# Six taps of a depthwise convolution on ScalarE, summed by adding transfers, and the convolution norm's sums placed later

## The chip, the cores and the metric

The kernel runs on one core of a Trainium2 chip. The metric is the device time of one execution in microseconds (us). For the kernel before, three runs gave 868.67, 869.35 and 869.78 us; the median is 869.35. A further execution was recorded by the hardware profiler, and all profile lines come from it. The engines are called PE (TensorE; PEld is its weight load), DVE (VectorE), ACT (ScalarE), POOL (GpSimd) and SP (the queue that loads the weights).

## The reference

One decoder layer on 512 tokens of width 1024, in float32: a half-weighted SwiGLU feed-forward, a mixing part, and a second feed-forward. The mixing part projects the normalized input and splits it over three groups: sliding-window attention (8 heads of 64, window 128), a convolution group, and cross-attention into 256 memory tokens (4 heads). Their outputs are joined, multiplied by `w_out` and added to the input. The change is in the convolution group, which has 256 channels and 31 taps:

```python
def conformer_conv(u, w_dw, b_dw, g_ln, b_ln):
    a, gate = jnp.split(u, 2, axis=-1)
    h = a * jax.nn.sigmoid(gate)
    h = lax.conv_general_dilated(
        h, w_dw[:, None, :].astype(h.dtype), window_strides=(1,),
        padding=((CONV_WIDTH - 1, 0),), dimension_numbers=('NWC', 'WIO', 'NWC'),
        feature_group_count=CONV_CH) + b_dw
    return jax.nn.silu(layer_norm(h, g_ln, b_ln))
```

Per channel, the output at token t is the sum over the taps j of `w_dw[j]` times `h[t - 30 + j]`, plus a bias. The layer norm runs over the 256 channels.

## The kernel before

Activations are kept transposed: channels lie on the 128 partitions, the 512 tokens along the free axis. Each float32 matrix product is made of three matmuls on split operands (high x high, high x low, low x high). ACT writes the high part of each weight block and DVE the low part, from a buffer that SP's queue fills (the class `Weights`).

The mixing part is written out by hand. The string `ORDER` lists its steps; a loop calls them in that order. `pM0`, `pK`, `pS2` and so on project one tile of queries, keys or values; `sumX` and `facX` make the factors of the head norms; `scoresXj`, `softXj`, `weightsX`, `turnXj` and `valuesX` are one attention unit's parts; `outD_K` adds the products of output block D with the head pairs K. A list scheduler then orders the instructions on each engine, so steps that stand next to each other can interleave; each engine runs its own queue strictly in that order.

The convolution runs between these steps. The 256 channels are two halves (i = 0, 1) of 128 partitions. `glu(i, ...)` writes the gated input to `pad[:, i]`, with 30 zeros ahead of it (line 794 of the profile). `taps()` is a generator: its first call makes tap 0 of both halves (line 799), each later call one tap of both halves on DVE, `conv[:, i] = pad shifted by j * w + conv[:, i]` (line 805). The step `c` in `ORDER` calls it once by `pump(1)`. What is left is made at `ln_mean`, which calls `pump(TAPS)`.

The norm has four steps. `ln_mean` adds the two halves (line 1066), takes the mean over the channels by a matmul with a matrix of 1/256 (line 1068) and subtracts it (line 1070). `ln_square` squares on ACT (line 1076) and adds on DVE (line 1078). `ln_var` sums over the channels by matmuls of one column (line 1083), takes the reciprocal square root in small DVE operations and spreads it (line 1089). `ln_swish`, called after the third block of the next loop, transposes the spread factor (line 1037), multiplies (1095), applies the gain, the bias and the swish (1096) and splits the result (lines 972 and 973). `valuesS3`, the last step of `ORDER`, makes the last head pair's output (line 956).

A transfer that adds to its destination is there already in the feed-forward parts: four times in each, a product is scaled into a work tile on ACT and POOL's queue adds it to `x` (lines 504 and 505). Transfers of this kind are issued from POOL's queue; an engine that needs the sum waits for the landing. Softmax probabilities, turned by 90 degrees, lie in tiles from `pttile()`, a set of eight buffers of 128 x 512.

Of the kernel before, what the change touches and what calls it, by code (L numbers as in the profile page):

```python
# [34 lines left out]
AF = mybir.ActivationFunctionType  # L35
ALU = mybir.AluOpType
# [3 lines left out]
T = 512  # L40
# [6 lines left out]
TAPS = 31  # L47
# [4 lines left out]
C_BDW, C_GLN, C_BLN = 36, 38, 40  # L52
C_WDW = 42
# [9 lines left out]


ORDER = """
c c c c pM0 sumM0 pM1 sumM1 c c facM pK c scoresM00 scoresM01 c softM01 softM00 weightsM0 c sumK c pV scoresM11
scoresM10 turnM00 turnM01 softM10 c softM11 weightsM1 facK c valuesM0 normK turnV c ropeK c turnM10 turnM11
pS0 ropeS0 sumS0 pS1 sumS1 facA ropeS1 c valuesM1 pS2 scoresS01 scoresS00 softS00 softS01 c weightsS0 ropeS2 sumS2 c
pS3 scoresS10 softS10 scoresS11 out0_01 sumS3 out1_01 facB c turnS00 turnS01 softS11 scoresS20 c weightsS1 c c
valuesS0 turnS10 scoresS21 softS20 out1_2 ropeS3 softS21 c c turnS11 weightsS2 c valuesS1 scoresS30  # L70
turnS20 scoresS31 out0_2 softS31 turnS21 softS30 out2_0123 out1_3 weightsS3 c c out0_3 valuesS2 c c out3_0123 c
ln_mean ln_square turnS30 ln_var out4_0123 turnS31 out5_0123 valuesS3
""".split()
TILES = [s[1:] for s in ORDER if s[0] == "p"]

# [5 lines left out]
N_ACT = 20  # L81

SUM_BUFS = 3
MEM_F = 17
B_T3, B_Q1, B_Q2, B_T4, B_21, B_22, B_11 = range(7)


class Weights:
# [33 lines left out]
    def make_sums(self, i):  # L122
        nc = self.nc
        g, u = self.raw[i], self.raw[i + 1]
        s12 = self.extra.tile([P, 1024], F32, tag="sum", name=f"s12_{i}", bufs=SUM_BUFS)
        s43 = self.extra.tile([P, 1024], F32, tag="sum", name=f"s43_{i}", bufs=SUM_BUFS)
        l, r = slice(0, 512), slice(512, 1024)
# [56 lines left out]
    def next(self):  # L184
        i = self.at
        self.at += 1
        self.split_to(i + 1 + self.conv_ahead)
        return self.split.pop(i)
# [21 lines left out]
def layer(tc, ctx, a):  # L210
# [10 lines left out]
    def nm(s):  # L221
        uid[0] += 1
        return f"{s}_{uid[0]}"
# [172 lines left out]
    def ffn(pool, norm, first, gain, hooks, next_gain, last):  # L396
# [335 lines left out]
    hooks = {9 + i: [part] for i, part in enumerate(rotary())}  # L732
    hooks[MEM_F - 3] = [lambda: load(0), lambda: load(1)]
    hooks[MEM_F - 2] = [lambda: piece(0), lambda: piece(1), lambda: load(2), lambda: load(3)]
    hooks[MEM_F - 1] = [lambda: piece(2), lambda: piece(3)]
    hooks[MEM_F], hooks[MEM_F + 1] = [sums, p1], [p2]
    with tc.tile_pool(name="fast1", bufs=1) as pool:
        norm = ffn(pool, norm, STARTS, C_G1, hooks, C_GM, False)

    with tc.tile_pool(name="mix", bufs=1) as mix:  # L740
        norm = mixing(tc, nc, a, mix, W, norm, locals())
# [5 lines left out]
def mixing(tc, nc, a, mix, W, norm, e):  # L747
    PE, ACT, DVE, POOL = nc.tensor, nc.scalar, nc.vector, nc.gpsimd
    mm_bank, sc_bank, tp_bank, work, small = (e[n] for n in ("mm_bank", "sc_bank", "tp_bank", "work", "small"))
    par, ident, x, rb, rtok, rtok2 = (e[n] for n in ("par", "ident", "x", "rb", "rtok", "rtok2"))  # L750
# [8 lines left out]
    pad = mix.tile([P, 2, T + 32], F32, name="pad")  # L759
    conv = mix.tile([P, 2, T], F32, name="conv")  # L760
    kT = mix.tile([P, T], F32, name="kT")
# [16 lines left out]
    def pttile():  # L778
        return mix.tile([P, T], F32, tag="pt", name=nm("pt"), bufs=8)
# [8 lines left out]
    def glu(i, ps_a, ps_g):  # L788
# [4 lines left out]
        DVE.tensor_tensor(t2, ps_a, rb, op=ALU.mult)  # L793
        DVE.tensor_tensor(pad[:, i, 30 : 30 + T], t2, t, op=ALU.mult)

    def taps():
        w = lambda i, j: par[:, C_WDW + i * TAPS + j : C_WDW + i * TAPS + j + 1]
        for i in range(2):
            DVE.tensor_scalar(
                conv[:, i], pad[:, i, 0:T], w(i, 0), par[:, C_BDW + i : C_BDW + i + 1], op0=ALU.mult, op1=ALU.add  # L800
            )
        yield
        for j in range(1, TAPS):
            for i in range(2):
                DVE.scalar_tensor_tensor(conv[:, i], pad[:, i, j : j + T], w(i, j), conv[:, i], op0=ALU.mult, op1=ALU.add)
            yield

    tap = taps()

    def pump(n):  # L810
        for _ in range(n):
            next(tap, None)
# [29 lines left out]
    def rope(q):  # L842
        s = work()
        u = work()
        DVE.stream_shuffle(s, q, list(range(8, 16)) + list(range(0, 8)) + list(range(16, 32)))
        DVE.tensor_tensor(s, s, sinb, op=ALU.mult)
        DVE.tensor_tensor(u, q, cosb, op=ALU.mult)
        DVE.tensor_tensor(q, u, s, op=ALU.add)
# [156 lines left out]
    def sums(name, t, n):  # L1005

        if t == 0:
            v["st" + name] = small(8 * n)
        tile_name = name if name == "K" else GROUPS[name][t]
        head_sums(v["sq" + tile_name], v["st" + name][:, 8 * t : 8 * t + 8])  # L1010
# [49 lines left out]


    def ln_mean():
        pump(TAPS)
        both, avg = work(), work()[:, :P]
        POOL.memset(avg, 1.0 / 256.0)
        DVE.tensor_tensor(both, conv[:, 0], conv[:, 1], op=ALU.add)
        mean = tp_bank()
        PE.matmul(mean, avg, both, start=True, stop=True)
        for i in range(2):
            DVE.tensor_tensor(conv[:, i], conv[:, i], mean, op=ALU.subtract)  # L1070
# [20 lines left out]
    def ln_swish():  # L1091
# [7 lines left out]
    units = {"M0": 0, "M1": 1, "S0": 2, "S1": 3, "S2": 4, "S3": 5}  # L1099
    steps = {  # L1100
        "sumK": lambda: sums("K", 0, 1), "facK": key_factor, "normK": key_norm, "turnV": value_turn,
        "ropeK": lambda: rope(kT), "c": lambda: pump(1),
        "ln_mean": ln_mean, "ln_square": ln_square, "ln_var": ln_var,
    }
    for g, tiles in GROUPS.items():
# [127 lines left out]
```

## Time and profile before

| | |
|---|---|
| median of three runs | 869.35 us (868.67 to 869.78) |
| profiled execution, its time | 871.94 us |
| its span, first to last instruction | 870.1 us |
| mean granted PE clock | 0.998 |
| busy: PE, DVE, ACT, POOL | 862.3, 700.9, 446.3, 32.3 us |
| convolution taps on DVE (line 805) | 60 of 743 ns, from 390.0 to 491.8 us |
| the mixing part | about 376 to 545 us |

Times in the profile are counted from the first instruction of the span. In a timeline row stand the start, the time to the end of the last of the merged instructions, the engine, the line, the operation, what it writes and reads, the shape, and the count; in brackets, how long the engine idled before it and what ended that. Matmuls are pipelined: each is shown with its full time, so two that overlap both count, and a busy PE can still be waiting a little. In a group row the numbers behind the bar are the busy time in us and the mean of one in ns.

### The profile page before, as it was taken

How to read it: one execution, taken by the hardware profiler on the slowest of the kernel's cores; microseconds unless marked ns; L12 is line 12 of the kernel's file. 1: busy time of each engine (PE TensorE's matmuls, PEld its weight loads, DVE VectorE, ACT ScalarE, POOL GpSimd, SP SyncE). 2: the span in 40 equal slices, each digit the busy share in tenths (PEclk: the TensorE clock that was granted, in tenths of full speed). 3: DMA queues.
4: the chain of work that ended last, by engine and by line, in shares of the span. 5: the costliest groups of instructions: out<-in, count | busy, mean ns of one | idle time of the engine just before them, and what ended most of it. 6: DMA issues, size and time to landing. Idle time of an engine off the chain costs nothing.

```text
span 870.1 us, 14858 instructions
## 1 busy us (share of the span) xinstructions
PE 862.3 (99%) x5929; PEld 777.5 (89%) x5929; DVE 700.9 (81%) x1163; ACT 446.3 (51%) x739; POOL 32.3 (4%) x31
## 2 busy tenths in 40 slices
PE   9999999999999999999999999999999999999998
PEld 5889999999999998888777778889999999999998
DVE  7998878897888876769999876997987878787772
ACT  7455545454564444532949654454554444545540
POOL 0010000000120000300000021010000000000000
PEclk9999999999999999999999999999999999999999
DMA  7326334333334334222010412335334333324312
GB/s 272 121 83 166 94 96 133 98 99 120 121 122 145 107 108 131 73 96 61 13 49 13 134 56 91 98 90 161 100 111 121 98 113 90 115 96 117 103 49 98
DMA packets 34373, 90.60 MB, mean 104 GB/s; under 512 B 3200, under 2 KB 5760, under 8 KB 34304
## 3 DMA queue, kind: packets, MB, share of 16 engines
q1 hardware_dynamic: 32000, 85.99, 31.7%
q0 software_dynamic: 1152, 2.10, 1.5%
q10 hardware_dynamic: 1152, 1.57, 0.5%
q8 instruction: 46, 0.75, 0.3%
q14 instruction: 23, 0.19, 0.1%
HBM read 85.45 MB, written 2.10 MB: 101 GB/s over the span
## 4 chain that ended last, share of the span: by engine, by line
PE 95%; ACT 2%; DVE 1%; DMA 1%; issue 0%; SPq 0%; ACTq 0%
PE mm L350 15%; PE mm L349 15%; PE mm L351 15%; PE mm L446 11%; PE mm L448 11%; PE mm L447 11%; PE sc L446 2%; PE sc L448 2%; PE sc L447 2%; PE sc L349 1%; PE sc L350 1%; PE sc L351 1%; PE tp L956 1%; ACT p L907 1%; PE tp L942 1%; DMA x<-in_xT 1%
## 5 line engine op out<-in xcount | busy, mean ns | idle before, releaser
L446 PE MATMUL mm<-bh,whi 128*128 128x256 f32 x864 | 239.9, 278 | 0.0
L448 PE MATMUL mm<-bh,wlo 128*128 128x256 f32 x864 | 239.6, 277 | 0.0
L447 PE MATMUL mm<-bl,whi 128*128 128x256 f32 x864 | 239.6, 277 | 0.0
L169 ACT CAST whi<-wraw 128x1024 fp32r<-128x1024 f32 (+2 forms) x122 | 124.1, 1021 | 108.5 <-PE mm L350 48.8
L170 DVE TENSOR_TENSOR wlo<-wraw,whi 128x1024 fp32r<-128x1024 f32 (+2 forms) x122 | 145.2, 1192 | 35.3 <-ACT whi L169 34.9
L447 PEld LDWEIGHTS mm<-bl,whi 128*128 128x128 f32 x864 | 163.1, 189 | 0.7
L446 PEld LDWEIGHTS mm<-bh,whi 128*128 128x128 f32 x864 | 162.3, 188 | 0.7
L448 PEld LDWEIGHTS mm<-bh,wlo 128*128 128x128 f32 x864 | 162.2, 188 | 0.0
L351 PE MATMUL mm<-hh,wlo 128*128 128x256 f32 (+1 forms) x496 | 161.3, 326 | 0.0
L350 PE MATMUL mm<-hl,whi 128*128 128x256 f32 (+1 forms) x496 | 161.2, 326 | 0.0
L349 PE MATMUL mm<-hh,whi 128*128 128x256 f32 (+1 forms) x496 | 160.6, 326 | 0.0
L170 DVE TENSOR_TENSOR wlo<-s,whi 128x1024 fp32r<-128x1024 f32 x72 | 87.9, 1222 | 32.4 <-ACT whi L169 32.1
L351 PEld LDWEIGHTS mm<-hh,wlo 128*128 128x128 f32 x496 | 93.2, 188 | 9.2
L350 PEld LDWEIGHTS mm<-hl,whi 128*128 128x128 f32 x496 | 93.2, 188 | 8.0
L349 PEld LDWEIGHTS mm<-hh,whi 128*128 128x128 f32 x496 | 93.2, 188 | 7.9
L169 ACT CAST whi<-s 128x1024 fp32r<-128x1024 f32 x72 | 75.5, 1050 | 47.3 <-PE mm L447 43.5
L349 PE MATMUL mm<-xh,whi 128*128 128x512 f32 x192 | 76.2, 401 | 0.3 <-ACT whi L181 0.2
L350 PE MATMUL mm<-xl,whi 128*128 128x512 f32 x192 | 75.8, 395 | 0.5 <-DVE xl L361 0.5
L351 PE MATMUL mm<-xh,wlo 128*128 128x512 f32 x192 | 75.7, 394 | 0.0
L508 DVE SCALAR_TENSOR_TENSOR x<-mm,x 128x512 f32<-128x512 f32 x80 | 54.0, 683 | 4.0 <-PE mm L351 4.0
L169 ACT CAST vhi<-wraw 128x512 fp32r<-128x512 f32 x36 | 22.4, 622 | 59.6 <-PE sc L447 47.2
L467 ACT ACTIVATE t<-t 128x512 f32<-128x512 f32 x36 | 22.8, 633 | 56.3 <-DVE t L466 56.2
(243 smaller groups left out, 1378.8 us busy)
## 6 DMA issues: line engine op xcount, KB each, us to landing
wraw<-in_wgu SPq DMA_DIRECT2D x86, 512.0 KB, 3.5
wraw<-in_wd SPq DMA_DIRECT2D x44, 512.0 KB, 3.7
wraw<-in_win SPq DMA_DIRECT2D x12, 512.0 KB, 3.5
x<-t POOLq DMA_DIRECT2D x8, 256.0 KB, 6.2
out<-t SPq DMA_DIRECT2D x7, 256.0 KB, 2.0
x<-in_xT SPq DMA_DIRECT2D x3, 512.0 KB, 6.5
wraw<-in_wout_a SPq DMA_DIRECT2D x6, 256.0 KB, 2.7
wraw<-in_wgu SPq DMA_DIRECT2D x4, 256.0 KB, 4.9
```

The source lines that it names most:

```text
L169: nc.scalar.copy(hi[:, :cols], raw[:, :cols])
L170: nc.vector.tensor_tensor(lo[:, :cols], raw[:, :cols], hi[:, :cols].bitcast(F32), op=ALU.subtract)
L349: PE.matmul(ps[:, t], wh[:, w], hi(k)[:, t], start=one, stop=False, skip_group_check=cut > 1)
L350: PE.matmul(ps[:, t], wh[:, w], lo(k)[:, t], start=False, stop=False, skip_group_check=cut > 1)
L351: PE.matmul(ps[:, t], wl[:, w], hi(k)[:, t], start=False, stop=end, skip_group_check=cut > 1)
L446: PE.matmul(ps, wh[:, c], bh[k][:, block], start=one, stop=False, skip_group_check=not first)
L447: PE.matmul(ps, wh[:, c], bl[k][:, block], start=False, stop=False, skip_group_check=not first)
L448: PE.matmul(ps, wl[:, c], bh[k][:, block], start=False, stop=end, skip_group_check=not first)
L467: ACT.activation(g, g, AF.Silu)
L508: DVE.scalar_tensor_tensor(o, ps, 0.5, xd, op0=ALU.mult, op1=ALU.add)
L907: ACT.activation(self.p[n, h][:, c], src[h][:, i, c], AF.Exp, scale=self.fac[:, m : m + 1], bias=self.neg[:, m : m + 1], accum_out=self.de ...
L942: PE.transpose(ps[:, i * P : (i + 1) * P], self.p[n, h][:, c : c + P], ident)
```

## The change

Taps 0 to 5 of the second half go from DVE to ACT. Tap 0 with the bias is written to `conv[:, 1]`, tap 1 to a tile of the `pt` set; taps 2 to 5 are each written to a `pt` tile of their own and added by a transfer from POOL's queue, the even ones to `conv[:, 1]`, the odd ones to tap 1's tile. A fifth transfer adds that tile to `conv[:, 1]`. DVE's taps 6 to 30 of the second half then go on from `conv[:, 1]`. DVE's generator now yields single taps, first the whole first half and then the second; `c` takes two of them. A new step `a` makes one of ACT's taps; six `a` stand at the head of `ORDER`. At its end, `ln_square` stands behind `turnS30`, and `ln_var` behind `out5_0123`.

```diff
-c c c c pM0 sumM0 pM1 sumM1 c c facM pK c scoresM00 ...
+a a a c a c a a c c pM0 sumM0 pM1 sumM1 c c facM pK c scoresM00 ...
...
-ln_mean ln_square turnS30 ln_var out4_0123 turnS31 out5_0123 valuesS3
+ln_mean turnS30 ln_square out4_0123 turnS31 out5_0123 ln_var valuesS3
...
+N_ADDED = 6
...
     def taps():
-        w = lambda i, j: par[:, C_WDW + i * TAPS + j : C_WDW + i * TAPS + j + 1]
-        for i in range(2):
-            DVE.tensor_scalar(
-                conv[:, i], pad[:, i, 0:T], w(i, 0), par[:, C_BDW + i : C_BDW + i + 1], op0=ALU.mult, op1=ALU.add
-            )
-        yield
-        for j in range(1, TAPS):
-            for i in range(2):
-                DVE.scalar_tensor_tensor(conv[:, i], pad[:, i, j : j + T], w(i, j), conv[:, i], op0=ALU.mult, op1=ALU.add)
+
+        for i, j in [(0, j) for j in range(TAPS)] + [(1, j) for j in range(N_ADDED, TAPS)]:
+            w, src = tap_weight(i, j), pad[:, i, j : j + T]
+            if (i, j) == (0, 0):
+                DVE.tensor_scalar(conv[:, i], src, w, par[:, C_BDW : C_BDW + 1], op0=ALU.mult, op1=ALU.add)
+            else:
+                DVE.scalar_tensor_tensor(conv[:, i], src, w, conv[:, i], op0=ALU.mult, op1=ALU.add)
             yield

-    tap = taps()
+    def added_taps():
+
+        chains = [conv[:, 1], pttile()]
+        for j in range(N_ADDED):
+            w, src = tap_weight(1, j), pad[:, 1, j : j + T]
+            if j == 0:
+                ACT.activation(chains[0], src, AF.Identity, scale=w, bias=par[:, C_BDW + 1 : C_BDW + 2])
+            elif j == 1:
+                ACT.activation(chains[1], src, AF.Copy, scale=w)
+            else:
+                o = pttile()
+                ACT.activation(o, src, AF.Copy, scale=w)
+                POOL.dma_start(chains[j % 2], o, accum_op=ALU.add)
+            if j == N_ADDED - 1:
+                POOL.dma_start(chains[0], chains[1], accum_op=ALU.add)
+            yield
+
+    tap, added = taps(), added_taps()
...
-        pump(TAPS)
+        pump(2 * TAPS)
...
-        "c": lambda: pump(1),
+        "c": lambda: pump(2), "a": lambda: next(added, None),
```

POOL's queue, between the squares' sums ahead of the mixing part and the norm's matrix, has five new rows in the changed kernel (its lines lie up to 19 further down). What each waits for stands in brackets; `pt_4155` is tap 1's tile, DMASW is the landing of an earlier transfer of this queue:

```order
L822 DMA conv<-pt_4158 128x512 [waits Activation_49]
L822 DMA pt_4155<-pt_4163 128x512 [waits Activation_49]
L822 DMA conv<-pt_4168 128x512 [waits DMASW4_49,Activation_49]
L822 DMA pt_4155<-pt_4171 128x512 [waits DMASW5_49,Activation_49]
L824 DMA conv<-pt_4155 128x512 [waits DMASW7_49,DMASW6_49,DMASW0_49]
```

The third waits for the first, the fourth for the second, and the fifth for both of these.

DVE's queue at the factor of the memory queries (`facM`, the small operations on `qfac` and `s`), before:

```order
L334 TENSOR_SCALAR qfac_4250<-s_4198 128x16 [waits DVE_49]
L335 TENSOR_SCALAR s_4253<-s_4198 128x16
L805 SCALAR_TENSOR_TENSOR conv<-pad,par,conv 128x512
L337 TENSOR_TENSOR s_4254<-qfac_4250 128x16 [waits DVE_49]
L805 SCALAR_TENSOR_TENSOR conv<-pad,par,conv 128x512
L338 TENSOR_TENSOR s_4254<-s_4254,s_4253 128x16 [waits DVE_49]
```

And in the changed kernel:

```order
L335 TENSOR_SCALAR qfac_4266<-s_4214 128x16 [waits DVE_49]
L336 TENSOR_SCALAR s_4269<-s_4214 128x16
L807 SCALAR_TENSOR_TENSOR conv<-pad,par,conv 128x512 [waits DVE_49]
L338 TENSOR_TENSOR s_4270<-qfac_4266 128x16 [waits DVE_49]
L807 SCALAR_TENSOR_TENSOR conv<-pad,par,conv 128x512 [waits DMASW0_49]
L339 TENSOR_TENSOR s_4270<-s_4270,s_4269 128x16 [waits DVE_49]
```

The small operations keep their places. The tap between the first two products is now tap 6 of the second half, and it waits for the landing of the fifth adding transfer.

PE's queue at the end of `ORDER`, from the mean's matmul on. Before (`sc_5285` and `sc_5317` are the output blocks 4 and 5, the rows with `ident` are transposes):

```order
L1068 MATMUL tp_5234<-t_5230,t_5231 128x512
L942 MATMUL tp_5243<-ident,p_5130 128x128 x3
L942 MATMUL tp_5243<-ident,p_5104 128x128
L350 MATMUL mm_5211<-yl_3976,whi_5205 128x512
L351 MATMUL mm_5211<-yh_3968,wlo_5206 128x512
L349 MATMUL sc_5285<-yh_3968,whi_5279 128x512
L350 MATMUL sc_5285<-yl_3976,whi_5279 128x512
L942 MATMUL tp_5250<-ident,p_5104 128x128 x3
L351 MATMUL sc_5285<-yh_3968,wlo_5280 128x512
...
L1083 MATMUL tp_5256<-ones,t_5240 128x1 x4
```

And in the changed kernel, the rows ahead of the variance sums:

```order
L351 MATMUL mm_4856<-yl_3976,whi_5221 128x512
L961 MATMUL tp_5285<-ident,p_5149 128x128 x3
L961 MATMUL tp_5285<-ident,p_5123 128x128
L352 MATMUL mm_4856<-yh_3968,wlo_5222 128x512
L961 MATMUL tp_5292<-ident,p_5123 128x128 x3
L350 MATMUL mm_4875<-yh_3968,whi_5221 128x512
L351 MATMUL mm_4875<-yl_3976,whi_5221 128x512
L352 MATMUL mm_4875<-yh_3968,wlo_5222 128x512
L350 MATMUL mm_5164<-yh_3968,whi_5221 128x512
L351 MATMUL mm_5164<-yl_3976,whi_5221 128x512
L352 MATMUL mm_5164<-yh_3968,wlo_5222 128x512
L1102 MATMUL tp_5317<-ones,t_5263 128x1 x4
```

Before, 8 matmuls of 512 columns and 7 transposes stand between the mean's matmul and the variance sums; now 13 and 14. The mean's matmul now stands among the first products of output block 5, the variance sums behind the third of the next loop's blocks.

More of the change, by code (lines that the diff above doesn't have):

```diff
@@ L65 @@
 ORDER = """
-c c c c pM0 sumM0 pM1 sumM1 c c facM pK c scoresM00 scoresM01 c softM01 softM00 weightsM0 c sumK c pV scoresM11
+a a a c a c a a c c pM0 sumM0 pM1 sumM1 c c facM pK c scoresM00 scoresM01 c softM01 softM00 weightsM0 c sumK c pV scoresM11
 scoresM10 turnM00 turnM01 softM10 c softM11 weightsM1 facK c valuesM0 normK turnV c ropeK c turnM10 turnM11
@@ L794, in glu, with tap_weight @@
         DVE.tensor_tensor(pad[:, i, 30 : 30 + T], t2, t, op=ALU.mult)
+    def tap_weight(i, j):
+        return par[:, C_WDW + i * TAPS + j : C_WDW + i * TAPS + j + 1]
     def taps():
-        w = lambda i, j: par[:, C_WDW + i * TAPS + j : C_WDW + i * TAPS + j + 1]
-        for i in range(2):
-            DVE.tensor_scalar(
-                conv[:, i], pad[:, i, 0:T], w(i, 0), par[:, C_BDW + i : C_BDW + i + 1], op0=ALU.mult, op1=ALU.add
-            )
-        yield
-        for j in range(1, TAPS):
-            for i in range(2):
-                DVE.scalar_tensor_tensor(conv[:, i], pad[:, i, j : j + T], w(i, j), conv[:, i], op0=ALU.mult, op1=ALU.add)
-            yield
-    tap = taps()
+        for i, j in [(0, j) for j in range(TAPS)] + [(1, j) for j in range(N_ADDED, TAPS)]:
[4 more added lines that the diff above has]
+                DVE.scalar_tensor_tensor(conv[:, i], src, w, conv[:, i], op0=ALU.mult, op1=ALU.add)
+            yield
+    def added_taps():
[14 more added lines that the diff above has]
+    tap, added = taps(), added_taps()
     def pump(n):
@@ L1101, in mixing @@
         "sumK": lambda: sums("K", 0, 1), "facK": key_factor, "normK": key_norm, "turnV": value_turn,
-        "ropeK": lambda: rope(kT), "c": lambda: pump(1),
+        "ropeK": lambda: rope(kT), "c": lambda: pump(2), "a": lambda: next(added, None),
         "ln_mean": ln_mean, "ln_square": ln_square, "ln_var": ln_var,
```

## The prediction

> **What bounds the kernel now.** I read the page first, then TensorE's waits, then tables by stage (busy time of PE, PEld, DVE, ACT, POOL with counts, granted clock, share of the DMA engines, GB/s), and last the instructions around the places that the change touches.
>
> ```profile
> PE 862.3 (99%) x5929; PEld 777.5 (89%) x5929; DVE 700.9 (81%) x1163; ACT 446.3 (51%) x739; POOL 32.3 (4%) x31
> PE tp L1083 <- DVE t L1078: 1.4, 1, 1.4
> PE tp L956 <- ACT pt L945: 0.5, 2, 0.3
> 390.00:410.00 20.00, 20.00 (x107) 16.13 (x107) 18.82 (x37) 6.58 (x10) 0.00 (x0) 1.00 0.18 54
> 490.00:510.00 20.00, 18.06 (x101) 13.91 (x100) 12.40 (x28) 9.15 (x14) 0.00 (x0) 0.91 0.32 93
> ```
>
> TensorE sets the end: it is busy 99% of the span. A change on VectorE or ScalarE is therefore worth only what it takes from, or adds to, TensorE's waits. The longest of them in this part is the 1.4 us in which the convolution norm's variance sums (L1083) wait for VectorE's sum of squares (L1078). It lies in the only stage of the middle part with a granted clock under 1.0 (0.91 over 490 to 510 us). The instructions there, of TensorE and VectorE, and four stretches of 3.4 us:
>
> ```profile
> 482.99 1.75 PE L956 MATMUL tp<-pt,vtok 128*64 128x128 f32 x28
> 494.17 1.02 PE L1068 MATMUL tp<-t,t 128*128 128x512 f32 x2
> 495.92 1.27 DVE L1070 TENSOR_TENSOR conv<-conv,tp 128x512 f32<-128x512 f32 x2
> 498.49 0.69 DVE L1078 TENSOR_TENSOR t<-t,t 128x512 f32<-128x512 f32 x1 [1.30 <-ACT t L1076]
> 499.24 1.05 PE L1083 MATMUL tp<-ones,t 128*128 128x1 f32 x8 [1.41 <-DVE t L1078]
> 501.46 2.97 PE L956 MATMUL tp<-pt,vtok 128*64 128x128 f32 x28 [0.35 <-ACT pt L945]
> 495.00:498.40 3.40, 2.83 (x16) 2.00 (x14) 2.19 (x3) 2.06 (x4) 0.00 (x0) 1.00 0.92 264
> 498.40:501.80 3.40, 2.22 (x21) 1.98 (x23) 1.96 (x10) 1.03 (x3) 0.00 (x0) 1.00 0.26 104
> 501.80:505.20 3.40, 3.40 (x31) 3.04 (x27) 0.99 (x5) 0.71 (x2) 0.00 (x0) 0.50 0.02 5
> 505.20:508.60 3.40, 3.40 (x16) 2.51 (x15) 1.88 (x3) 2.79 (x3) 0.00 (x0) 1.00 0.00 0
> ```
>
> The reader is to see two losses. TensorE idles 1.41 us, then 0.35 us. Right behind a stretch with only 2.22 us of busy time out of 3.40 the clock is granted at 0.50 for 3.4 us, and the same 28 matmuls that took 1.75 us at 482.99 take 2.97. A half clock for 3.4 us costs 1.7 us of TensorE's time.
>
> **The change, part by part.** *The norm's sums are moved.* From the end of the mean's matmul (494.17 + 1.02 = 495.19) to L1083 at 499.24 the chain of two subtractions, two squares and a sum takes 4.05 us. In the new order 13 matmuls of 512 columns and 14 transposes stand between the two. The cadences come from these rows: one 512-column matmul starts 0.23 us after the other, and eight transposes take 0.87 us on the chain.
>
> ```profile
> 485.01 0.40 PE L349 MATMUL mm<-yh,whi 128*128 128x512 f32 x1
> 485.24 0.39 PE L350 MATMUL mm<-yl,whi 128*128 128x512 f32 x1
> 422.42 0.87 PE tp L942 x8
> ```
>
> 13 x 0.23 + 14 x 0.11 = 4.5 us, more than the 4.05: the wait of 1.4 us goes, and with it most of the 0.35 (I take 0.2). The next thing late is the last windowed head pair and the norm's own output: its values are followed at once by matmuls on their low part, which need a cast and a subtraction (some 0.5 us beyond the four matmuls ahead), and less work stands ahead of the norm's output than before. I give back 0.4 us. Idle time: -1.4 - 0.2 + 0.4 = -1.2. If the thin stretch is gone, the half clock is too: -1.7. Together **-2.9 us**.
>
> *Six taps leave VectorE.* They are six of these, spaced 0.66 us (five in 3.40):
>
> ```profile
> 398.53 3.40 DVE L805 SCALAR_TENSOR_TENSOR conv<-pad,par,conv 128x512 f32<-128x512 f32 x5
> 388.34 0.55 DVE L799 TENSOR_SCALAR conv<-pad,par 128x512 f32<-128x512 f32 x1
> 387.61 0.69 DVE L794 TENSOR_TENSOR pad<-t,t 128x512 f32<-128x512 f32 x1 [1.44 <-ACT t L791]
> ```
>
> That takes off 6 x 0.66 = 4.0 us of VectorE. Some of it comes back: the taps of one half now often follow one another, and a dependent instruction starts 0.04 us behind the end of the one before (387.61 + 0.69 = 388.30, then 388.34) where independent ones overlap by 0.08: 0.12 us more for each of some ten such places, 1.2 us. The rest, 2.8 us, pays for nothing by itself, since TensorE's waits hardly name VectorE; it is what lets the mean stand 14 matmuls earlier. If it were missing, the mean would be late instead.
>
> *Six ScalarE activations are added*, 0.71 us by the nearest row (0.82 for the one with a bias), spaced about 0.62 since ScalarE's activations overlap by 0.1. The second half of the padded input is written at 390.66 + 0.68 = 391.34, and ScalarE idles from there to 393.96:
>
> ```profile
> 390.66 0.68 DVE L794 TENSOR_TENSOR pad<-t,t 128x512 f32<-128x512 f32 x1
> 393.96 1.06 ACT L169 CAST whi<-wraw 128x1024 fp32r<-128x1024 f32 x1 [3.75 <-PE mm L350]
> 394.92 0.59 ACT L817 ACTIVATE t<-mm 128x512 f32<-128x512 f32 x1
> L360 ACT ACTIVATE xh<-x,par 128x512 fp32r<-128x512 f32 x8 | 5.7, 710 | 0.0
> L1096 ACT ACTIVATE conv<-conv,par 128x512 f32<-128x512 f32 x2 | 1.6, 816 | 0.2 <-DVE conv L1095 0.2
> ```
>
> All six end near 395.4. The square at 394.92 slips by 0.4 us, behind which VectorE already waited 1 us for TensorE's sums; I price it at 0. Without that idle stretch it would cost 3.8 us of ScalarE.
>
> *Five adding transfers of 256 KB, in two chains*, come onto POOL's queue; POOL runs nothing from 390 to 410 us. This is the term that decides. The last transfer adds one chain to the other, so three landings follow one another, and VectorE's tap 6 of the second half waits for the third. In VectorE's new order that tap stands between two small operations of a factor, where now a tap starts at 405.56:
>
> ```profile
> 405.47 0.16 DVE L337 TENSOR_TENSOR s<-qfac 128x16 f32<-128x16 f32 x1
> 405.56 0.74 DVE L805 SCALAR_TENSOR_TENSOR conv<-pad,par,conv 128x512 f32<-128x512 f32 x1
> 406.22 0.16 DVE L338 TENSOR_TENSOR s<-s,s 128x16 f32<-128x16 f32 x1
> 413.67 1.28 ACT L907 ACT_TABLE_LOAD   x1 [4.54 <-DVE neg L898]
> 408.04 1.03 PE L871 MATMUL mm<-mk,q 64*128 64x256 f32 x8
> 415.60 1.74 PE L871 MATMUL mm<-mk,q 64*128 64x256 f32 x8
> 418.67 1.13 PE L871 MATMUL sc<-mk,q 64*128 64x256 f32 x4
> ```
>
> Behind it on VectorE stand the factor, four maxima and the negated maxima (L898); for these ScalarE's softmax waits (4.54 us already), and for its exponentials TensorE's next scores: the eight matmuls at 415.60 take 1.74 us where eight at 408.04 take 1.03, so TensorE waits 0.7 us there already. No slack is left in that chain: each us that the transfer is late is a us of TensorE.
>
> The landing times come from the accumulating transfers of the feed-forward parts, the same size, kind and queue: all eight, then the first and the second of the group at 583 us alone.
>
> ```profile
> DMA to landing us min/median/max: 3.4/6.2/8.2
> DMA to landing us min/median/max: 3.4/3.4/3.4
> DMA to landing us min/median/max: 5.0/5.0/5.0
> 583.40 1.80 POOL L505 DMA_DIRECT2D x<-t  x2 [52.70 <-DVE bl L439]
> ```
>
> A transfer alone lands after 3.4 us, the second of a pair (issued 0.9 later) after 5.0, the third and fourth after up to 8.2, since four are queued there. Here two at most are in flight. The first addend is ready at 391.34 + 0.8 + 2 x 0.65 + 0.1 = 393.6; issues at 393.7 and 394.6; the second lands at 394.6 + 5.0 = 399.6; its successor meets one nearly finished transfer, so I take 3.7, nearer the lone row: 403.4; the last is alone: 403.5 + 3.5 = **407.0**, 1.4 us after 405.56. Bounds: 3.4 each gives 394.6 + 3 x 3.5 = 405.1, not late; 5.0 each gives 409.9, 4.3 late; the median 6.2 each gives 413.5, 7.9 late.
>
> *A second-order cost of that wait.* With 1.4 + 0.7 us, and the 0.6 us lost in the scores at 418.67 (four in 1.13 us, where eight took 1.03), the stretch around 416 would be about as thin as the one at 498.40 (1.76 us idle and small matmuls), behind which the clock was halved. I take +1.7; its bounds are 0 and 1.7.
>
> The Trainium skill ("TensorE: Matmul & The Clock Gate", Part 1) has the clock halved after a window of about 3.4 us in which the array idled. The row at 498.40 has 2.22 us of busy time in such a window and the next is still at 0.50, so here the page's rule is too mild; by the rule neither wait would halve the clock, and the new stall would come without its 1.7.
>
> Sum: -2.9 + 1.4 + 1.7 = **+0.2 us** on the profiled span of 870.1. That execution took 871.94, 2.6 above the median of the three runs shown (869.35); I carry the difference over unchanged: 869.5.
>
> **Rivals.** (1) *The transfers are in time.* For it: a lone transfer takes 3.4, and from 390 to 410 the DMA engines are a fifth busy. Against it: the pair's second took 5.0. Then nothing is paid: -2.9, 866.4. The Trainium skill ("DMA: Bandwidth & Descriptors", Anatomy of one DMA) fits such a transfer as about 2.0 us plus its bytes at 436 GB/s, an estimate of 2.6 us for 256 KB, by which the last would land near 402.7 and this rival would hold; none of the eight here landed under 3.4.
>
> (2) *The clock stays.* As the forecast, late by 1.4, but the stall falls across two of the clock's windows: -2.9 + 1.4 = -1.5, 867.9.
>
> (3) *The queue's latency decides: slower.* The second transfer of each pair waits for the first, as those at 583 us did, and all land after 5.0 or more. The tap is 4.3 us late, TensorE stops as long and loses a half clock: -2.9 + 4.3 + 1.7 = +3.1, 872.5; at the median, +6.7, 876.1. It decides from a lateness of about 3 us (landing behind 408.6). Against it: only two are in flight, and nothing else is on the queue.
>
> (4) *The norm's wait only moves.* If the transposes among the covering matmuls wait for their copies, or the mean itself is late since VectorE was, the 1.4 us and the half clock stay: without any lateness 0, with it up to +3.
>
> **How the numbers follow.** Forecast with its half clock 0.37; clock stays 0.12; in time 0.30; slow queue 0.16; norm unchanged 0.05. A measurement tells 0.2% (1.7 us) from no change: 867.6 to 871.1 is the same. Faster is rival 1 and some of rival 2 with a lateness under 1.2: 0.36. Slower is rival 3, half of rival 4 and the forecast's upper edge (late by over 3): 0.22. Same: 0.42. The range goes from rival 1 (866.4, less 0.2) to the slow queue with 5.0 each (872.5, plus 0.3), which leaves out the median-latency case and little else. The forecast's own range is 868 to 871.
>
> **What would show it.** Right: the wait of L1083 is under 0.3 us and the clock is 1.0 there; the fifth adding transfer lands about 1.4 us after VectorE is ready for tap 6, an idle time that names the adding transfer; TensorE's scores at some 417 wait about that much longer, with a granted clock of 0.5 behind them; the DMA view shows the new transfers at 3.4 to 5.0 us. Wrong: a landing before 405.6 (then rival 1), behind 408.6 (rival 3), full clock behind a stall of 1.4 us or more (rival 2), or an idle time of over 1 us that is still there ahead of the variance sums (rival 4).

## The result, and the profile after

The changed kernel takes 877.3 us (median of six runs, 875.33 to 881.49) where the kernel before, beside it, takes 868.1: ratio 1.0113, 95% interval 1.0087 to 1.0140. In a second comparison the ratio was 1.0082 (1.0058 to 1.0106). It is 7 to 9 us **slower**; the forecast was 869.5, with a range up to 872.8. The profiled execution took 879.11 us, with a span of 877.3.

The busy times on the page of the changed kernel moved by 5 us at most (PE +5.1 us, ACT +3.5, POOL +4.4, DVE -1.4), and do not say where the time went.

```profile
PE 867.4 (99%) x5929; PEld 781.0 (89%) x5929; DVE 699.5 (80%) x1157; ACT 449.8 (51%) x745; POOL 36.7 (4%) x36
```

TensorE's waits in the mixing part of the changed kernel say more (what waited and for what; total us, times, longest):

```profile
PE mm L890 <- ACT p L926: 3.1, 1, 3.1
PE mm L350 <- ACT yh L991: 1.6, 1, 1.6
PE tp L961 <- ACT p L948: 0.2, 1, 0.2
```

The 1.4 us ahead of the norm's variance sums is gone. In its place stand 3.1 us at the scores, for ScalarE's exponentials, and 1.6 us at the first matmuls that read the norm's output. By stage (busy time of PE, PEld, DVE, ACT, POOL with counts; granted clock, DMA share, GB/s), the changed kernel:

```profile
418.90:422.31 3.41, 1.44 (x6) 0.97 (x7) 3.41 (x10) 3.40 (x11) 0.00 (x0) 1.00 0.00 0
422.31:432.55 10.24, 10.24 (x27) 6.80 (x26) 7.38 (x21) 6.23 (x17) 0.00 (x0) 0.50 0.01 2
490.00:510.00 20.00, 20.00 (x139) 15.90 (x138) 16.91 (x39) 14.78 (x36) 0.00 (x0) 1.00 0.47 145
```

Behind a stretch in which TensorE was busy for 1.44 of 3.41 us, the clock is 0.50 for 10.24 us. In these TensorE is busy throughout at half the clock, so about half of them, 5.1 us, is lost. At the norm (490 to 510) the clock is 1.0 and nothing idles. TensorE's instructions that can be set against those of before:

```profile
416.31 0.40 PE L352 MATMUL mm<-xh,wlo 128*128 128x512 f32 x1
416.63 1.13 PE L890 MATMUL mm<-mk,q 64*128 64x256 f32 x4
420.87 1.13 PE L890 MATMUL mm<-mk,q 64*128 64x256 f32 x4 [3.11 <-ACT p L926]
424.12 2.07 PE L890 MATMUL sc<-mk,q 64*128 64x256 f32 x4
493.18 1.75 PE L975 MATMUL tp<-pt,vtok 128*64 128x128 f32 x28
517.71 1.19 PE L350 MATMUL mm<-yh,whi 128*128 128x512 f32 x4 [1.56 <-ACT yh L991]
```

Of the kernel before, one of these rows was shown, at 482.99; the two others:

```profile
415.27 0.40 PE L351 MATMUL mm<-xh,wlo 128*128 128x512 f32 x1
510.15 1.20 PE L349 MATMUL mm<-yh,whi 128*128 128x512 f32 x4 [0.34 <-ACT yh L972]
```

The last matmul of the value projection starts 1.04 us later than before (416.31 to 415.27). That comes from before the change: the matmuls of one column ahead of the mixing part, at 377.24 us, were at 376.10. The 28 value matmuls of the third pair are 10.19 late: the scores' stage cost **+9.15**. The first matmuls on the norm's output are 7.56 late: the norm's stage gained **2.63**. The eight scores at the stop take from 416.63 to 422.00 us, 5.37 us, where the eight at 415.60 took 1.74: 3.63 more. What is left of the 9.15, 5.5 us, comes behind them, nearly all of it the 5.1 us of the low clock; there, scores four at a time take 2.07 us where they took 1.13.

What TensorE waits for there is late because VectorE was. POOL's queue, VectorE and ScalarE in the changed kernel:

```profile
394.86 0.89 POOL L822 DMA_DIRECT2D conv<-pt  x1 [25.24 <-ACT pt L821]
395.48 1.17 POOL L822 DMA_DIRECT2D pt<-pt  x1
400.06 0.86 POOL L822 DMA_DIRECT2D conv<-pt  x1 [3.41 <-DMA conv<-pt]
402.19 0.86 POOL L822 DMA_DIRECT2D pt<-pt  x1 [1.26 <-DMA pt<-pt]
406.35 0.86 POOL L824 DMA_DIRECT2D conv<-pt  x1 [3.30 <-DMA pt<-pt]
409.67 0.75 DVE L807 SCALAR_TENSOR_TENSOR conv<-pad,par,conv 128x512 f32<-128x512 f32 x1 [2.95 <-DMA conv<-pt]
418.32 1.28 ACT L926 ACT_TABLE_LOAD   x1 [8.17 <-DVE neg L917]
```

VectorE waits 2.95 us for the fifth transfer. The softmax starts 4.65 us later than before (413.67 there), 3.6 beyond the offset of 1.04, which is what the scores lose at the stop.

### The profile page after: what moved, and what is told of

Same layout as the page of the kernel before. It is cut to its first block, busy times and chain, and to the rows that moved or that the text cites. A ratio compares the mean times of both kernels' runs of the same rounds, so it can differ in the third digit from the quotient of the medians.

```text
span 877.3 us, 14873 instructions
## 1 busy us (share of the span) xinstructions
PE 867.4 (99%) x5929; PEld 781.0 (89%) x5929; DVE 699.5 (80%) x1157; ACT 449.8 (51%) x745; POOL 36.7 (4%) x36
## 3 DMA queue, kind: packets, MB, share of 16 engines
q0 software_dynamic: 1872, 3.41, 2.4%
## 4 chain that ended last, share of the span: by engine, by line
PE 93%; DMA 2%; DVE 2%; ACT 2%; issue 1%; SPq 0%; POOL 0%; POOLq 0%; ACTq 0%
PE mm L350 15%; PE mm L351 15%; PE mm L352 15%; PE mm L449 11%; PE mm L447 11%; PE mm L448 11%; PE sc L449 2%; PE sc L447 2%; PE sc L448 2%; PE sc L350 1%; PE tp L961 1%; PE sc L351 1%; PE sc L352 1%; DMA pt<-pt 1%; PE sc L890 1%; DMA x<-in_xT 1%
```

## The experiments

Two executions of one and the same kernel differ in the first feed-forward part: the last value-projection matmul of the changed kernel started at 416.31 in one trace and at 411.32 in another. So besides the ratio, each table row below has the time from that matmul to the end of the span, in one profiled execution, against the 454.8 us of before (870.1 - 415.27).

| kernel | ratio to before (95%) | from the scores to the end |
|---|---|---|
| changed, second comparison | 1.0082 (1.0058 to 1.0106) | +7.5 |
| norm's order alone | 1.0024 (1.0008 to 1.0039) | +2.1 |
| taps alone | 1.0051 (1.0037 to 1.0065) | +5.7 |
| no joining transfer | 1.0048 (1.0030 to 1.0065) | +6.6 |
| extra matmuls in the stop | 1.0040 (1.0026 to 1.0055) | +3.3 |
| own buffer, old norm order | 0.9986 (0.9969 to 1.0003) | -3.6 |
| own buffer, new norm order | 0.9987 (0.9972 to 1.0003) | -3.6 |
| one chain, new norm order | 0.9981 (0.9966 to 0.9995) | -2.6 |
| four taps, old norm order | 1.0036 (1.0017 to 1.0056) | +5.1 |
| one chain, old norm order | **0.9952 (0.9934 to 0.9970)** | -4.3 |

**Theory** after the first traces: the wait for the last landing, and the low clock behind it, are the loss; the norm's part is a gain. **Rivals**: the added work on ScalarE and the DMA engines is the loss; or the moved sums are.

### The norm's order alone

```diff
 # the kernel before
-ln_mean ln_square turnS30 ln_var out4_0123 turnS31 out5_0123 valuesS3
+ln_mean turnS30 ln_square out4_0123 turnS31 out5_0123 ln_var valuesS3
```

> The kernel before with the new order of the norm's steps alone: all taps stay on VectorE, no adding transfer. Theory (the move of the sums is a gain of its own, the added taps are the loss): the 1.4 us wait of the variance sums and the half clock behind it go, 2.9 us less, ratio 0.9967; granted clock 1.0 between 490 and 510 us. Rival (the move needs the lighter VectorE, or the wait only moves): within 1 us of before, ratio 0.999 to 1.001, with an idle time of over 1 us still ahead of the variance sums or a stretch at 0.5 behind them.

Measured: 1.0024, **slower by 2.1 us**. TensorE's three longest waits in the mixing part of this kernel:

```profile
PE mm L349 <- ACT yh L972: 2.7, 1, 2.7
PE tp L1037 <- DVE t L1089: 1.1, 1, 1.1
PE tp L1083 <- ACT pt L945: 0.6, 1, 0.6
```

The wait for the square is gone, and the later variance makes its factor (L1089) late by 1.1 and the norm's output (L972) by 2.7 us. The half clock moved too (by stage, the same kernel):

```profile
508.77:512.18 3.41, 3.41 (x10) 2.65 (x9) 1.74 (x4) 0.73 (x1) 0.00 (x0) 0.50 0.09 23
```

So the theory's gain does not come from the order. The rival of the prediction, that the wait only moves, holds for this part by itself.

### The taps alone

```diff
 # the changed kernel
-ln_mean turnS30 ln_square out4_0123 turnS31 out5_0123 ln_var valuesS3
+ln_mean ln_square turnS30 ln_var out4_0123 turnS31 out5_0123 valuesS3
```

> The changed kernel with the norm's steps back in their old order: the six taps by ScalarE and adding transfers stay. Theory (late chain and clock are the loss): the 3.1 us stop of TensorE ahead of its scores and the half clock behind it stay; the 2.6 us that the norm's move gained are lost: 9.2 + 2.6, about 12 us slower than before, ratio 1.0135. Rival (the move of the sums costs, the taps are harmless): not slower than before, ratio under 1.002. Rival (ScalarE's and the DMA engines' added work spread over the whole stage is the loss): about as slow, but with no wait of TensorE over 2 us at the scores.

Measured: 1.0051, 4.4 us slower, and not the 12 expected. TensorE in this kernel:

```profile
415.44 2.07 PE L890 MATMUL mm<-mk,q 64*128 64x256 f32 x4 [3.02 <-ACT p L926]
489.20 1.75 PE L975 MATMUL tp<-pt,vtok 128*64 128x128 f32 x28
496.94 1.02 PE L1087 MATMUL tp<-t,t 128*128 128x512 f32 x2
502.15 1.05 PE L1102 MATMUL tp<-ones,t 128*128 128x1 f32 x8
512.02 1.08 PE L350 MATMUL mm<-yh,whi 128*128 128x512 f32 x4
```

The stop at the scores is the same, 3.02 us. But in the norm's stage TensorE no longer waits at all: from the 28 value matmuls to the first on the norm's output it gains 6.21 - 1.87 = **4.3 us** on the kernel before, where the changed kernel gained 2.6. The chain from mean to variance is as long as ever (497.96 to 502.15, 4.19 us, where it was 4.05); what changed is that the mean's matmul stands earlier, 7.74 us behind the row of the value matmuls (496.94 - 489.20) where it was 11.18 (494.17 - 482.99), since VectorE has six taps less to do ahead of it (it is 11.19 with the new order alone and 7.75 in the changed kernel, so the taps do it, not the order); more of the output matmuls are left to fill the chain. The order alone (+2.1) and the taps alone (+4.4) add up to 6.5, about the 7.1 of the second comparison.

### Without the joining transfer

```diff
 # the changed kernel
+    late = rb
...
-        chains = [conv[:, 1], pttile()]
+        chains = [conv[:, 1], late]
...
-            if j == N_ADDED - 1:
-                POOL.dma_start(chains[0], chains[1], accum_op=ALU.add)
...
 def ln_mean():
+    DVE.tensor_tensor(conv[:, 1], conv[:, 1], late, op=ALU.add)
```

(`rb` is the spread factor of the norm ahead of the mixing part, not needed any more here.)

> The changed kernel without the fifth adding transfer (the one that joins the two chains): the second chain is added by one VectorE sum ahead of the mean. All six activations and four of five transfers stay. Theory (only the wait for the last landing costs, and the half clock that it brings): VectorE's first tap of the second half now needs only the first chain, whose second landing came some 2 us before VectorE was ready; the stop of TensorE shrinks to the 0.7 us of before, no half clock there, and the gain at the norm is left: 2 to 3 us less than before, ratio 0.9965 to 0.998, some 11 us less than the changed kernel. Rival (the added ScalarE work and the transfers cost by themselves): still over 5 us slower than before. A first chain that lands late by its own would show as an idle time of VectorE that names it.

Measured: 1.0048, 4.2 us slower than before and some 3 us better than the changed kernel, not 11. By itself that is nearer the rival. The trace shows why it does not decide: VectorE and TensorE in this kernel (here the scores are L889):

```profile
399.35 1.42 DVE L808 SCALAR_TENSOR_TENSOR conv<-pad,par,conv 128x512 f32<-128x512 f32 x2 [2.33 <-DMA conv<-pt]
415.39 1.98 PE L889 MATMUL mm<-mk,q 64*128 64x256 f32 x4 [2.17 <-ACT p L925]
```

The landing comes earlier, but so does the tap that waits: the scheduler reckons with the landing and now puts it as the 11th of VectorE's taps instead of the 15th. VectorE idles 2.33 us instead of 2.95, TensorE 2.17 instead of 3.11, and 13.65 us at 0.50 follow. Four of its seven runs had a mean clock of 1.0 and still took 869.2 to 873.4 us, so the low clock is not its whole loss. What counts is then the landing *against the place of the tap that waits*, which the kernels below test.

### Extra matmuls in the stop

```diff
 # the changed kernel, in scores()
+N_BUSY = 14
...
-            for i in range(2):
+            busy = not self.win and self.t == 1 and j == 1
+            if busy:
+                junk = tp_bank()
+            for i, h in [(i, h) for h in range(2) for i in range(2)] if busy else [(i, h) for i in range(2) for h in range(2)]:
                 n = 2 * j + i
                 c = self.cols(n)
-                for h in range(2):
+                if busy and (i, h) == (0, 1):
+                    for _ in range(N_BUSY):
+                        PE.matmul(junk, xhk(0)[:, :P], xhk(0), start=True, stop=True)
...
```

The edit also puts these scores in order of the head, so that the four of the first head stand ahead of the extra matmuls.

> The changed kernel with 14 extra matmuls of 512 columns (3.2 us, their result is not used) on TensorE in the middle of the scores that wait, so that the wait of 3.1 us is as long as before but TensorE is not idle in it. The landing is as late as in the changed kernel. Theory (two losses: a wait of 3.1 us, and a half clock of three windows, 5.1 us, that TensorE's idleness brings): the extra matmuls cost nothing, the half clock goes or shrinks to one window: 3.4 to 6.8 us less than the changed kernel, ratio to before 1.0035 to 1.0075. Rival (the low clock has another cause, or the slow scores are slow because ScalarE is late): no gain, ratio 1.0105 or more, with stretches at 0.5 still between 415 and 435 us.

Measured: 1.0040, 3.6 us less than the changed kernel, with 3.47 us of work added. TensorE, and then the stages, of this kernel:

```profile
418.31 3.47 PE L893 MATMUL tp<-xh 128*128 128x512 f32 x14
421.71 1.13 PE L897 MATMUL mm<-mk,q 64*128 64x256 f32 x4
423.62 0.70 PE L897 MATMUL sc<-mk,q 64*128 64x256 f32 x2 [0.78 <-ACT p L933]
```

```profile
418.90:425.74 6.84, 5.66 (x25) 3.68 (x23) 6.84 (x20) 6.83 (x19) 0.00 (x0) 1.00 0.00 0
425.74:432.57 6.83, 6.01 (x24) 5.24 (x23) 6.83 (x17) 4.77 (x12) 0.00 (x0) 0.50 0.01 2
```

The stop is filled, the low clock comes 3.4 us later and lasts two windows of 3.41 us, not three or four. All runs bear this out: five of these six have a mean clock of 0.996, which is two windows, where eleven of the changed kernel's twelve have 0.992 or 0.994. Waiting and low clock are two losses, and the second follows from the stop. It is not gone, since the smaller waits behind (0.78, 0.40, 0.82 us) remain.

### The landing taken out of the queue, with both orders of the norm

```diff
 # the changed kernel; once with the norm's old order, once with the new
+    late = rb
...
+            elif (i, j) == (1, N_ADDED):
+                DVE.tensor_scalar(late, src, w, None, op0=ALU.mult)
             else:
-                DVE.scalar_tensor_tensor(conv[:, i], src, w, conv[:, i], op0=ALU.mult, op1=ALU.add)
+                acc = late if i else conv[:, 0]
+                DVE.scalar_tensor_tensor(acc, src, w, acc, op0=ALU.mult, op1=ALU.add)
...
 def ln_mean():
+    DVE.tensor_tensor(conv[:, 1], conv[:, 1], late, op=ALU.add)
```

> The changed kernel with the norm's steps in their old order, and with VectorE's taps of the second half in a buffer of their own; the chain of ScalarE's taps is added to them by one VectorE sum ahead of the mean. All six activations and all five transfers stay, but no tap waits for a landing. Theory (the wait for the last landing and the half clock behind it are the loss, the lighter VectorE is a gain at the norm, the new order costs 2 us): no stop at the scores over the 0.7 us of before, no idle time at the norm; the 4.4 us gained there in the kernel with the taps alone, less up to 0.7 for the extra sum: 3.5 to 4.5 us faster than before, ratio 0.995 to 0.996. Rival (the added work on ScalarE and on the DMA engines is the loss): 3 to 5 us slower than before, as with the taps alone.

> The same buffer of its own for VectorE's taps of the second half, with the norm's new order. Theory: as the kernel with the old order, but 1.6 to 2 us slower, since the norm's output is late for the last matmuls (an idle time of 1 to 2 us that names the split of the norm's output): 1.5 to 2.9 us faster than before, ratio 0.9965 to 0.998. Rival (the new order is a gain as predicted, 1.2 us of idle time): faster than the kernel with the old order.

Measured: 865.87 and 866.61 us where before has 868.68; ratios 0.9986 and 0.9987, just short of certain. All six activations and all five transfers are still there, and nothing is lost by them: the rival of the added work falls. TensorE at the scores (here L894), with the old norm order:

```profile
414.48 1.13 PE L894 MATMUL mm<-mk,q 64*128 64x256 f32 x4 [0.65 <-ACT p L930]
```

The stop is 0.65 us, and this execution had no low clock. It is on the edge: of the twelve runs of the kernel with the old order, eight granted a mean clock of 1.0 and took 865.0 to 866.1 us; four granted 0.992 to 0.994 and took 869.0 to 871.2. A mean of 0.994 is three windows at half speed, as in the trace of the changed kernel. Between the two norm orders nothing is to be told here; the scheduler placed other work differently as well, and both have a last wait of 0.2 us. The expected 1.6 to 2 us did not show, and the 3.5 to 4.5 us of gain expected with the old order shows on the trace (-3.6) and not in the ratio, which includes the runs with a low clock.

### One chain instead of two

```diff
 # the changed kernel
-                POOL.dma_start(chains[j % 2], o, accum_op=ALU.add)
+                POOL.dma_start(chains[0], o, accum_op=ALU.add)
```

> The changed kernel with all four adding transfers into the first chain, so that five landings follow one another instead of three: at 3.4 us and 0.45 to the next issue each, the last lands near 414 us instead of 409.6, and VectorE's tap, one operation later in its order, waits about 7 us instead of 2.95. Theory (each us of lateness is a us of TensorE): the stop at the scores grows from 3.1 to about 7 us, the stretch at 0.5 behind it stays 10 to 14 us: 4 us slower than the changed kernel, ratio to before 1.012 to 1.016. Rival (lateness does not set the end, the added work does): as slow as the changed kernel within 1 us.

Measured: 0.9981, **faster**, where 4 us more were expected. The landings came even later than reckoned; POOL's first and last issue and VectorE in this kernel:

```profile
390.92 0.89 POOL L822 DMA_DIRECT2D conv<-pt  x1 [25.26 <-ACT pt L821]
409.13 0.86 POOL L824 DMA_DIRECT2D conv<-pt  x1 [3.22 <-DMA conv<-pt]
410.81 0.23 DVE L917 TENSOR_TENSOR neg<-s,qnfac 128x4 f32<-128x4 f32 x2
412.45 1.41 DVE L807 SCALAR_TENSOR_TENSOR conv<-pad,par,conv 128x512 f32<-128x512 f32 x2 [0.66 <-DMA conv<-pt]
```

From first to last issue it is 18.2 us, where the changed kernel took 11.5 (394.86 to 406.35): 6.7 us more, where 4.4 were reckoned. But the scheduler, seeing the long chain, put the tap that waits *behind* the maxima and the negated maxima (L917). The expectation had assumed a place one operation later; the tap went six taps later. A landing 7 us later, counted from the first issue, costs nothing: TensorE's scores, 2.02 us for eight, no longer wait for it. That is the clearest answer to the prediction's "each us that the transfer is late is a us of TensorE". What TensorE still waits for in the mixing part is the norm's output, 1.3 us.

### Four taps

```diff
 # the changed kernel, with the norm's old order
-N_ADDED = 6
+N_ADDED = 4
```

> Four taps by ScalarE instead of six, so three transfers (two chains of one, then the joining one), with the norm's steps in their old order. Two landings follow one another instead of three, so the last lands some 4 us earlier than in the changed kernel. But the scheduler, which reckons with landings too, now puts the tap that waits earlier too: 12th of VectorE's taps instead of 15th. From the traces: first issue 390.9, the second of the pair lands 6.2 after its issue, near 397.7, the joining one 0.45 + 3.3 later near 401.4; VectorE is ready for its 12th tap near 397. Theory (what counts is the landing against the place of the waiting tap in VectorE's queue, ahead of the maxima): VectorE waits 3.5 to 4.5 us, TensorE stops 3 to 4 us at the scores with a stretch at 0.5 behind it: 4 to 6 us slower than before, ratio 1.0045 to 1.007. Rival (an earlier landing and less added work are what counts): no stop, ratio under 0.999.

Measured: 1.0036, slower. POOL, VectorE and TensorE in this kernel:

```profile
397.99 0.86 POOL L824 DMA_DIRECT2D conv<-pt  x1 [5.16 <-DMA pt<-pt]
401.29 1.42 DVE L807 SCALAR_TENSOR_TENSOR conv<-pad,par,conv 128x512 f32<-128x512 f32 x2 [3.10 <-DMA conv<-pt]
416.14 2.07 PE L890 MATMUL mm<-mk,q 64*128 64x256 f32 x4 [2.19 <-ACT p L926]
```

Fewer transfers, landed at 401.3 as reckoned, and VectorE waits as long as in the changed kernel (3.10 us), because the tap that waits stands that much earlier. The waits are under the expected ones (3.10 where 3.5 to 4.5 were expected, 2.19 where 3 to 4), and so is the ratio (1.0045 or more was expected); the sign is as expected, and the rival of the earlier landing falls.

### One chain and the old order of the norm

The edits of the last but one kernel and of the taps alone, together.

> All adding transfers in one chain, as in the kernel that was 0.19% faster than before, and the norm's steps in their old order. On all engines the order up to the norm is the same as there. Theory (the new order of the norm's steps costs some 1.5 us, since the norm's output comes late for the last matmuls): the wait of 1.3 us for the split of the norm's output goes, 1 to 1.7 us faster than with the new order: 865.0 to 865.7 us, ratio 0.996 to 0.997. Rival (the order of the norm's steps makes no difference once VectorE is lighter, as the pair with the buffer of its own showed within 0.7 us): ratio 0.998 to 0.9985.

Measured: 864.31 us where before has 869.01, ratio **0.9952 (0.9934 to 0.9970)**: 4.2 us faster than before, the best of all and a little more than expected. TensorE and VectorE of this kernel:

```profile
413.03 1.42 DVE L807 SCALAR_TENSOR_TENSOR conv<-pad,par,conv 128x512 f32<-128x512 f32 x2 [0.16 <-DMA conv<-pt]
413.78 2.03 PE L890 MATMUL mm<-mk,q 64*128 64x256 f32 x8
```

The view of TensorE's waits names none from 374 to 525 us, neither at the scores nor at the norm. The new order of the norm costs 2 to 3 us in all three pairs where the instructions up to the norm are the same: alone (1.0024), with two chains (1.0082 against 1.0051) and with one (0.9981 against 0.9952), though the intervals of the last two pairs overlap a little.

## Why the prediction was wrong

**The step that failed is the price of the clock**: "I take +1.7; its bounds are 0 and 1.7". It held that a low clock lasts one window of 3.4 us, as the one window in the trace of before does. Measured were three windows here, 10.24 us at 0.50, 5.1 us lost; 13.65 us, 6.8 lost, in the second trace of the same kernel. The chance of a low clock was seen, its price was three to four times too small, and so the range ended at 872.8. With the measured lateness and the old price the sum would have been -2.9 + 2.95 + 1.7 = +1.75, 871.1 us and inside the range; with 5.1 for the clock it is 874.5 and outside. The runs of other kernels that came with and without the low clock agree on its size: medians of 870.1 and 865.4 us with the buffer of its own and the old order, 872.8 and 869.4 with four taps. And of the changed kernel's twelve runs the only one with a mean clock of 0.998, as of one window, took 871.29 us, inside the range, where the others took 874.65 to 881.49; a single run, so a sign and no proof. That the Trainium skill ("TensorE: Matmul & The Clock Gate", Part 1) would leave the clock alone at gaps under some 3.4 us was rightly set aside: a 3.41 us stretch with 1.44 us of busy time was enough. By the same section a busy window of that length brings the full clock back; here 10.24 us in which TensorE was busy throughout did not.

**The lateness was mis-sized too**: 1.4 us forecast, 2.95 measured, inside its bounds (0 to 4.3). Of the terms, "issues at 393.7 and 394.6" and the ready time of VectorE hold within 0.2 us, but for the offset of 1.04. The second of the first pair landed 6.2 us after its issue (395.48, the wait ended 401.7), where 5.0 was taken; the issue behind a landing follows after some 0.4 to 0.5 us, where 0.1 was taken, twice. Transfers and landings of the two lines in the trace of the changed kernel (L822, then L824):

```profile
DMA to landing us min/median/max: 3.6/4.2/6.2
DMA to landing us min/median/max: 3.3/3.3/3.3
```

The five took 4.7, 6.2, 3.8, 3.6 and 3.3 us in order of issue. The estimate of 2.6 us that followed from the page "DMA: Bandwidth & Descriptors" (Anatomy of one DMA) of the Trainium skill is under all of them. Rival 1 is excluded by the landing at 409.6. That landing is 408.6 without the offset of 1.04, just the bound that the text gives for rival 3 ("behind 408.6", late by about 3): what came lies on the border between the forecast and rival 3. Rival 3's own mechanism, that "all land after 5.0 or more", did not come; one of the five did.

**Each us late is a us of TensorE** held for this place of the tap: the softmax started 3.6 us late, of which the wait for the landing is 2.95, and the scores lost 3.6. As a rule it is wrong, as one chain shows: it holds as long as the tap stands ahead of the maxima.

**The norm's gain** was forecast at 2.9, measured at 2.6: right in size and in where it shows (no wait of L1102, clock 1.0). But its working was wrong, so the agreement is luck. The sentence that six taps off VectorE pay "for nothing by itself" has it the wrong way round: the taps alone gain 4.3 there, the moved steps alone lose 2.1. The give-back of 0.4 was too small; the wait for the norm's output grew from 0.34 to 1.56. To that extent rival 4, that the wait only moves, held as well.

**The six activations at no cost** held: all six run in the kernels that are faster than before.

With the measured terms: -2.6 at the norm, and +9.15 at the scores, of which 5.1 are the clock, 3.6 the stop and 0.4 the rest behind it: +6.5 on the trace. The span grew by 7.2: these 6.5 and the 1.04 ahead of the change, less 0.4 behind it.

## What to carry to other kernels

Where an engine's queue is strictly in order, ask first what stands behind the instruction that will wait, and only then how late its data is: here a chain of landings 7 us longer was free, and the shorter ones were not, because the scheduler moved the waiting tap with them. When the bounding engine has stretches that are nearly thin enough for a low clock, price the low clock by several windows, not one, and judge the stretch by what it streams, not by its busy time (last section). And keep two parts of a change apart: half of this one was a gain of 4 us that the other half, and a stop elsewhere, hid.

## What was not expected of the hardware

A low clock can last over several windows in which TensorE is busy. Stretches of some 3.4 us with 1.44, 1.24 and 0.78 us of busy TensorE were followed by three, four and four windows at 0.50, and the one with 2.22 us in the kernel before by a single one; the four values are from the changed kernel, the kernel without the joining transfer, the second trace of the changed kernel and the kernel before. The rows of the two that were not shown yet, first without the joining transfer:

```profile
412.12:415.53 3.41, 1.24 (x6) 0.78 (x6) 3.41 (x9) 2.67 (x6) 0.00 (x0) 1.00 0.00 0
415.53:429.18 13.65, 13.65 (x33) 9.08 (x34) 9.79 (x26) 8.39 (x23) 0.00 (x0) 0.50 0.00 1
```

and the second trace of the changed kernel:

```profile
412.00:415.36 3.36, 0.78 (x4) 0.34 (x2) 3.36 (x10) 1.95 (x4) 0.00 (x0) 1.00 0.00 0
415.36:429.01 13.65, 13.07 (x31) 8.69 (x32) 9.61 (x27) 8.40 (x24) 0.00 (x0) 0.50 0.01 1
```

Busy time does not tell which stretch brings a low clock. The 3.41 us around the wait for the norm's output, in the first trace of the changed kernel, are thinner than the 2.22 us of before, and the clock stays at 1.0:

```profile
514.47:517.88 3.41, 1.84 (x9) 1.22 (x8) 1.03 (x2) 3.40 (x5) 0.00 (x0) 1.00 0.41 129
517.88:521.30 3.42, 3.42 (x16) 2.79 (x17) 2.79 (x5) 1.52 (x3) 0.00 (x0) 1.00 0.19 36
```

What does tell is how many columns TensorE's matmuls stream. The clock changes only at whole windows of 3.41 us (10.24 is three, 13.65 four). Counting, in each window of all twelve traces, the columns of the matmuls that start in it (512 for a matmul shown as 128x512, one for a sum of one column), I get two limits without an exception in some 3000 windows. At full clock, the eight windows with 512 to 2304 columns were followed by half clock, and all the others, with 2696 or more, by full clock. At half clock, the fifteen windows with 2048 to 2816 columns were followed by another at half, and the eight with 3072 to 4096 by full clock. The 2.22 us of before hold 1672 columns, since many of those matmuls have one column or 128; the 1.84 us above hold 3584. That is why the low clock lasts behind the scores, as far as these counts go: at half clock a matmul of 512 columns starts each 0.43 us (0.23 at full clock), and four scores stream their 1024 columns in 2.07 us, less than half as many as such matmuls would, so a window with scores in it stays short of 3072. The count was made on these traces and no kernel varied it alone, so the limits are an estimate. Weighting the columns by the rows used (64 of 128 for the scores) separates the windows as well.

Why one and the same kernel sometimes gets the low clock and sometimes not (four of twelve runs of the kernel with the buffer of its own) is not settled. The windows lie differently in each execution: the last value matmul starts 0.83 us into its window in the first trace of the changed kernel and 2.79 in the second. So the same stop can fall into one window or be shared by two. That fits, but no run here tests it.
